# Query tiles and softmax reciprocals fetched by one 128-partition transfer each, with the queries' scratch rows laid out for it

## The chip, the core and the metric

The kernel runs on one core of a Trainium2 chip. The core has five engines that each run their own instruction list in order: TensorE (PE in the profile, with its weight loads shown apart as PEld), VectorE (DVE), ScalarE (ACT), GpSimd (POOL) and SyncE (SP). In this kernel SP computes nothing: it issues nearly every DMA, one after the other, and where a DMA has to wait for something, SP waits and all later DMAs stand behind it. The data of a DMA is then moved by 16 DMA engines that the whole core shares. The metric is the time on the device, in microseconds (us), as the median of 3 runs.

## What is computed

It is one step of a two-layer backbone on 1024 latent and 256 context tokens, 1280 in all, or ten tiles of 128 rows. Layer 0 is an attention layer, layer 1 a Fourier layer. Of the attention layer the following matters here:

```python
qa, ka, va, ga, qb, kb, vb, gb = split_even(h @ w_in)      # 8 q heads, 2 kv heads, head_dim 64, twice
qa = rms_norm(qa.reshape(b, s, A_HEADS, HEAD_DIM), gq)     # mixer A, then rotary positions
...
oa = dense_block_attention(qa, ...)                        # mixer A: all keys
ob = window_attention_with_ctx(qb, ..., sink)              # mixer B: +-128 tokens, context, sink
return jnp.concatenate([oa * jax.nn.silu(ga), ob * jax.nn.silu(gb)], axis=-1) @ w_out
```

A softmax divides by the sum of its exponentials. The kernel does not divide in the attention: it keeps the sums, turns them into reciprocals, and multiplies a whole row tile by reciprocals and gates just before the output projection.

## The kernel before

All matrix products run in a split format: an operand is kept as a high part and a low part, so one product is two or three matmuls. PE is the busy engine nearly everywhere.

The stretch that the change touches is layer 0, from the first query projections to the output projections.

**Queries out.** `q_pair` (from L773) makes the queries of two row tiles for one group of four heads. There are four groups `g` (0 and 1 of mixer A, 2 and 3 of mixer B) and five pairs of tiles, so twenty calls. After normalisation and rotary positions, its inner `post` transposes the result on PE, splits it into `qe` (high and low), and writes each of the two tiles to a scratch tensor in DRAM, `qd` (L185). The write at L803 takes 128 partitions of 512 numbers (2 KB). The partitions are two heads of 64 dimensions each, `(h d)`, and `qd` holds them in that order, `[NT, 4, 128, 512]`. There are 40 such writes.

**Queries in.** `load_q` (L926 to L930) fetches a tile's queries for one group. The keys occupy the 128 partitions as high part over low part (64 dimensions each), so the queries are wanted twice, once for each half of the partitions, and both heads side by side in a partition. Two transfers do that (L929): each fills 64 partitions with two rows of 2 KB. There are 40 tile loads, so 80 transfers. The buffers come from a zone named `q` with two places, which also lends places to `qe` and to other tiles. `attend` (from L1077) loads the next tile's queries during the first half of the present tile, so there is one tile of lookahead.

**Scores and weighing.** `soft` computes the scores of two heads at a time (L924, L996), `weigh` transposes the probabilities, multiplies by the values and writes the result to the scratch tensor `od` (L1064). Between these units a `Filler` hands out other PE work: the remaining projections and the gates. `totals` (L1012 on) writes the reciprocals of a tile to the scratch tensor `scd` (L1028).

**Into the output projection.** `proj_in` (from L1206) loads for one row tile the attention output (L1210), the gates (L1213) and the reciprocals (L1215). A reciprocal belongs to a head, and a head's 64 dimensions are 64 partitions, so the row of each of the two heads in a partition block is broadcast to 64 partitions, in two transfers of 64 rows of 4 KB. There are 10 row tiles, so 20 transfers.

The order of the instructions is not that of the code: a scheduler orders each engine's list ahead of time by its own model of durations. So the written form of a DMA can also move other instructions. The rows of `qd` and `scd` reach PE through these waits: a store into `qd` must have landed before its load is issued, a load must have landed before the tile's first score matmul, and a reciprocal load must have landed before the multiplication at L1216, on which the output projection rests.

Of the kernel before, what the change touches and what calls it, by code (L numbers as in the profile page):

```python
# [9 lines left out]
F32 = mybir.dt.float32  # L10
# [7 lines left out]
P = 128  # L18
D = 1024
NT = 10  # L20
# [119 lines left out]
def hybrid_step(ctx: ExitStack, tc: tile.TileContext, I, O):  # L140
    nc = tc.nc
    pe, act, dve, pool, sp = nc.tensor, nc.scalar, nc.vector, nc.gpsimd, nc.sync
# [3 lines left out]
    dr = ctx.enter_context(tc.tile_pool(name="dram", bufs=1, space=bass.MemoryType.DRAM))  # L146
# [9 lines left out]
    def take(tag, shape, dt=F32):  # L156
        tags = (tag,) if isinstance(tag, str) else tag
        z = min((t for t in tags if spare[t]), key=lambda t: spare[t][0])
        i = spare[z].popleft()[1]
        size = 2 if dt == BF16 else 4  # L160
        for s in shape[1:]:
            size *= s
        assert size <= 4 * ZONES[z][1]
        made[0] += 1
        return Buf(z, i, up.tile(list(shape), dt, tag=f"{z}{i}", name=f"{z}{made[0]}", bufs=1))

    def drop(*bufs):
        for b in bufs:
            stamp[0] += 1
            spare[b.zone].append((stamp[0], b.idx))  # L170

    def bank(tag, name, dt=F32):
        tag = ALIAS.get(tag, tag)
        return pp.tile([P, 512], dt, tag=tag, name=name, bufs=BANKS[tag])
# [7 lines left out]
        ring.rotate(-1)  # L182
        return bank(ring[-1], name)

    qd = dr.tile([NT, 4, P, 512], F32, name="qd")  # L185
    kd = dr.tile([2, P, NT * P], F32, name="kd")
    vd = dr.tile([2, NT, P, P], F32, name="vd")
    od = dr.tile([NT, P, 8, P], F32, name="od")
# [4 lines left out]
    scd = dr.tile([NT, 2, 8, P], F32, name="scd")  # L193
# [74 lines left out]
    def pick(key, cycle):  # L268
        turn[key] = turn.get(key, -1) + 1
        return {"d": dve, "p": pool, "a": act}[cycle[turn[key] % len(cycle)]]  # L270

    def copy(key, cycle, out, in_):
        e = pick(key, cycle)
        if e is act:
            act.activation(out, in_, AF.Copy)  # L275
        else:
            e.tensor_copy(out, in_)  # L277
# [395 lines left out]
    def transp(name, y, n):  # L673
        tp = t_bank(name)
        for i in range(n):
            pe.transpose(tp[:, i * P : i * P + P], y[:, i, :], ident)
        return tp
# [18 lines left out]
    def rope_pair(y, n, t, t1, t2):  # L696
        cb = rope[:, t : t + 2, 0:32].unsqueeze(2).to_broadcast([P, 2, 2 * n, 32])
        pick("rope", XE["rope"]).tensor_mul(  # L698
            t1.rearrange("p t h (b c) -> p t (h b) c", b=2), y.rearrange("p t h (b c) -> p t (h b) c", b=2), cb
        )  # L700
        for b in range(2):
            o, i = 32 * b, 32 - 32 * b
            sb = rope[:, t : t + 2, 32 + o : 64 + o].unsqueeze(2).to_broadcast([P, 2, n, 32])
            pick("rope", XE["rope"]).tensor_mul(t2[:, :, :, o : o + 32], y[:, :, :, i : i + 32], sb)
        pick("radd", XE["radd"]).tensor_add(t1, t1, t2)

    def norm_pair(name, src, y, sq, n, g, post=None):
        act.activation(sq, src, AF.Square)
        ss2 = sm.tile([P, 8], F32, tag="hssq", name=name + "ssq")[:, 0 : 2 * n]
        dve.tensor_reduce(out=ss2.rearrange("p (t h) -> p t h", t=2), in_=sq, op=ALU.add, axis=AX.X)  # L710
        rs = rsqrt(name + "rs", ss2, 2 * n, 1.0 / 64, post, pw=XE["pw"])
        rb = rs.rearrange("p (t h) -> p t h", t=2).unsqueeze(3).to_broadcast([P, 2, n, 64])
        dve.tensor_mul(y, y, rb)
        pick("gm", XE["gm"]).tensor_mul(y, y, g.unsqueeze(1).unsqueeze(1).to_broadcast([P, 2, n, 64]))

    def gemm_tok(acc, t, w, n=256):
        mm3(acc, [(*htile(t, k), *wk(w, k, 0, n)) for k in range(8)])
# [55 lines left out]
    def q_pair(m, kv, t, w, ptag, acc=None):  # L773
        if acc is None:
            acc = bank(ptag, f"q{m}{kv}{t}")
            for i in range(2):
                gemm_tok(acc[:, i * 256 : i * 256 + 256], t + i, w)
        yb = take(HZ[0], (P, 2, 4, 64))
        y = yb.a
        av = acc.rearrange("p (t h d) -> p t h d", t=2, h=4)  # L780
        act.activation(y, av, AF.Copy, scale=1.0 if m == 0 else 0.125)  # L781
        b1 = take(HZ[0], (P, 2, 4, 64))
        b2 = take(HZ[0], (P, 2, 4, 64))
        if m == 0:
            norm_pair(f"qn{kv}{t}", av, y, b2.a, 4, gq, 0.125)
        if t < 8:
            rope_pair(y, 4, t, b1.a, b2.a)
            y = b1.a
        if t < 8:
            drop(yb, b2)  # L790
            qb = b1
        else:
            drop(b1, b2)
            qb = yb

        def post():
            tp = transp(f"qT{m}{kv}{t}", y.rearrange("p t (a h) d -> p (t a) (h d)", h=2), 4)
            tv = tp.rearrange("p (t n) -> p t n", t=2)
            qe = take(QE_Z, (P, 2, 2, 256), F32R)
            copy("qev", E_QEV, qe[:, :, 0, :], tv)  # L800
            dve.tensor_sub(qe[:, :, 1, :], tv, qe[:, :, 0, :])
            for i in range(2):
                sp.dma_start(qd[t + i, 2 * m + kv], qe[:, i].rearrange("p a n -> p (a n)").bitcast(F32))  # L803
            drop(qe, qb)

        return post
# [118 lines left out]

    def load_q(t, g):  # L926
        q = take("q", (P, 2, 512))
        for i in range(2):
            sp.dma_start(q[64 * i : 64 * i + 64], qd[t, g].rearrange("(h d) f -> d h f", d=64))  # L929
        return q  # L930

    def soft(t, g, pr, qb):
# [140 lines left out]
    def flush_held(n=0):  # L1073
        while len(held) > n:
            held.popleft()()
# [59 lines left out]
    for i, nm in enumerate(order[:-1]):  # L1135
        j = int(nm[-1])
        work = []
        if nm[0] == "q":
            m = "ab".index(nm[1])
# [66 lines left out]
    def proj_in(src, gate, r, resid):  # L1206
        if gate is not None:
            flush_held()
            ol = take(OB[0], (P, 8, P))
            sp.dma_start(ol.a, src[r])  # L1210
            gl = take(OB[0], (P, 8, P))
            rl = take(OB[0], (P, 8, P))
            sp.dma_start(gl.a, gate[r])  # L1213
            for h in range(2):
                sp.dma_start(rl[64 * h : 64 * h + 64], scd[r, h].partition_broadcast(64))  # L1215
            pick("pm", XE["pm"]).tensor_mul(gl.a, gl.a, rl.a)  # L1216
            pick("pm", XE["pm"]).tensor_mul(ol.a, ol.a, gl.a)
            drop(gl, rl)
        hi, lo = take(OB[0], (P, 8, P), F32R), take(OB[0], (P, 8, P), F32R)
        if gate is not None:  # L1220
            split(hi.a, lo.a, ol.a, E_OH, E_OL)
            drop(ol)
        else:
            for c in range(2):
                split(hi[:, 4 * c : 4 * c + 4, :], lo[:, 4 * c : 4 * c + 4, :], src(c, r), "a", "d")
        xr = take(OB[0], (P, D))
        sp.dma_start(xr.a, resid[r * P : (r + 1) * P, :])
        return hi, lo, xr
# [426 lines left out]
    for n in range(4):  # L1655
        c, hf = divmod(n, 2)
# [306 lines left out]
```

## Time and profile before

| what | value |
|---|---|
| median of 3 runs (lowest to highest) | 1202.58 us (1201.54 to 1202.74) |
| the profiled execution's own time | 1202.03 us |
| its span, first to last instruction | 1200.2 us |
| PE busy | 1162.1 us, 97% of the span |
| DVE busy | 831.7 us, 69% |
| ACT busy | 578.5 us, 48% |
| POOL busy | 319.1 us, 27% |
| DMA: bytes moved, packets | 168.81 MB, 129840 |
| share of the 16 DMA engines' span taken by the SP queue's packets | 45.8% |

The profiled execution lies 0.55 us under the median, inside the spread of the runs. Between its time and its span there are 1.8 us that lie around the instructions. A share of DMA is a mean over the 16 engines: 0.45 of a stretch of 100 us means that each engine was busy for 45 us of it on average. The table gives averages over stages that differ much; the stretch from 100 to 830 us is the one with the attention layer.

### The profile page before, as it was taken

To read this page: it belongs to the slowest core of one execution; us is meant where nothing else is said; L and a number is where in the kernel's file an instruction comes from. 1 tells how busy PE (TensorE), PEld (TensorE's weight loads), DVE (VectorE), ACT (ScalarE), POOL (GpSimd) and SP (SyncE) were. 2 spreads that over 40 slices of the span, in tenths; PEclk is the share of its full clock that TensorE was granted. 3 is DMA by queue.
4 is the path that set the end of the run, shared out by engine and by line. 5 is a ranking of instruction groups with operands and counts; after the bars stand their busy time and mean duration, and the time that the engine had idled before them with its cause. 6 is when DMAs were issued, how large, how long until landed. Compare 5 with 4: busy or idle time off the path is not lost. (4 is left out here: it accounts for less than half of the span.)

```text
span 1200.2 us, 22028 instructions
## 1 busy us (share of the span) xinstructions
PE 1162.1 (97%) x8103; PEld 1038.7 (87%) x8103; DVE 831.7 (69%) x2000; ACT 578.5 (48%) x1159; POOL 319.1 (27%) x278
## 2 busy tenths in 40 slices
PE   7899899999999999999999979999999999999997
PEld 5787899999999999899988978888878888997886
DVE  3479688877677776678888957678756953467543
ACT  3343356665566555556666756433363224342211
POOL 2255554411322221010110113312212217345001
PEclk9899999999999999999999989999999999999999
DMA  9957512323623232354353587587114436264321
GB/s 316 370 188 255 162 52 64 113 76 88 169 69 104 75 95 76 90 127 123 79 151 80 159 232 223 184 253 248 54 45 158 137 110 181 86 206 147 123 105 54
DMA packets 129840, 168.81 MB, mean 141 GB/s; under 512 B 26298, under 2 KB 86454, under 8 KB 129732
## 3 DMA queue, kind: packets, MB, share of 16 engines
q1 hardware_dynamic: 129732, 167.40, 45.8%
q8 instruction: 64, 1.05, 0.4%
q14 instruction: 44, 0.36, 0.1%
HBM read 123.19 MB, written 44.16 MB: 139 GB/s over the span
## 5 line engine op out<-in xcount | busy, mean ns | idle before, releaser
L1044 DVE TENSOR_TENSOR pt<-pt,pt 128x512 fp32r<-128x512 f32 (+1 forms) x264 | 171.6, 659 | 45.0 <-ACT pt L275 44.2
L275 ACT ACTIVATE pt<-pt 128x512 fp32r<-128x512 f32 (+1 forms) x264 | 146.9, 575 | 95.8 <-PE pt L1041 56.7
L1047 PE MATMUL av<-pt,u 128*128 128x256 f32 x1008 | 165.6, 287 | 0.1
L1041 PE MATMUL pt<-identr,p 128*128 128x128 f32 x1008 | 154.6, 272 | 0.4 <-DVE pt L1044 0.3
L263 PE MATMUL q<-w,u 128*128 128x256 f32 x960 | 144.5, 288 | 0.2 <-ACT h L725 0.2
L1047 PEld LDWEIGHTS av<-pt,u 128*128 128x128 f32 x1008 | 138.1, 189 | 3.7 <-DVE pt L1044 0.8
L263 PEld LDWEIGHTS q<-w,u 128*128 128x128 f32 x960 | 127.5, 190 | 5.9 <-issue 0.8
L1041 PEld LDWEIGHTS pt<-identr,p 128*128 128x128 f32 x1008 | 118.9, 140 | 7.0 <-PE sB L996 0.9
L263 PE MATMUL ga<-u,w 128*128 128x512 f32 (+1 forms) x576 | 124.5, 360 | 0.3 <-DVE h L817 0.3
L965 ACT ACTIVATE p<-p,nm 128x1280 f32<-128x1280 f32 (+1 forms) x80 | 95.4, 1193 | 58.1 <-DVE p L958 57.8
L263 PEld LDWEIGHTS ga<-u,w 128*128 128x128 f32 x576 | 93.9, 188 | 14.5 <-ACT e L1056 0.5
L281 POOL TENSOR_TENSOR w<-h,w 128x512 fp32r<-128x512 f32 x39 | 52.3, 1357 | 129.6 <-DVE w L277 100.3
L924 PE MATMUL sL<-u,q 128*128 128x512 f32 x256 | 82.9, 411 | 0.3 <-DMA q<-qd 0.3
L281 POOL TENSOR_TENSOR u<-h,u 128x512 fp32r<-128x512 f32 x24 | 34.8, 1458 | 163.5 <-ACT u L275 151.9
L965 ACT ACTIVATE p<-p,NM 128x640 f32<-128x640 f32 (+2 forms) x80 | 59.1, 740 | 24.9 <-DVE p L958 24.5
L924 PE MATMUL sC<-u,q 128*128 128x256 f32 x320 | 63.4, 299 | 6.9 <-DMA q<-qd 6.6
L958 DVE TENSOR_SCALAR_CACHE_REDUCE p<-sL 128x512 f32<-128x512 f32 x64 | 43.9, 685 | 27.0 <-PE sL L924 17.5
L263 PE MATMUL oz<-u,u 128*128 128x512 f32 x208 | 59.6, 396 | 0.1
L263 PE MATMUL oz<-u,w 128*128 128x512 f32 x192 | 58.2, 395 | 0.0
L924 PEld LDWEIGHTS sC<-u,q 128*128 128x128 f32 x320 | 48.6, 191 | 9.7 <-issue 7.0
L958 DVE TENSOR_SCALAR_CACHE_REDUCE p<-sL,nm 128x512 f32<-128x512 f32 x64 | 47.7, 745 | 11.8 <-PE sL L924 10.9
L698 POOL TENSOR_TENSOR h<-h,rope 128x512 f32<-128x512 f32 (+1 forms) x18 | 21.6, 1199 | 125.7 <-ACT h L781 67.9
(738 smaller groups left out, 2568.5 us busy)
## 6 DMA issues: line engine op xcount, KB each, us to landing
q<-qd SPq DMA_DIRECT2D x80, 256.0 KB
p<-i_ada_w SPq DMA_DIRECT2D x20, 512.0 KB
h<-i_w_in SPq DMA_DIRECT2D x40, 256.0 KB
h<-i_w_out SPq DMA_DIRECT2D x32, 256.0 KB
pt<-i_ada_w SPq DMA_DIRECT2D x15, 512.0 KB
qd<-pt SPq DMA_DIRECT2D x20, 256.0 KB
q<-i_ada_w SPq DMA_DIRECT2D x9, 512.0 KB
qd<-q SPq DMA_DIRECT2D x18, 256.0 KB
```

The source lines that it names most:

```text
L263: pe.matmul(out, a, b, start=i == 0, stop=i == n - 1)
L275: act.activation(out, in_, AF.Copy)
L281: pick("lo" + lc, lc).tensor_sub(dst_l, src, dst_h)
L698: pick("rope", XE["rope"]).tensor_mul(t1.rearrange("p t h (b c) -> p t (h b) c", b=2), y.rearrange("p t h (b c) -> p t (h b) c", b=2), cb)
L924: pe.matmul(ps, q_at(q, s, hc), keys, start=s == 0, stop=s == 1)
L958: dve.tensor_scalar(p[i][:, end[i] : end[i] + n], ps, sign, last[i], op0=ALU.mult, op1=ALU.min, accum_out=c)
L965: act.activation(p[i][:, 0 : end[i]], p[i][:, 0 : end[i]], AF.Exp, bias=last[i], scale=-1.0, accum_out=SU[:, t, hd + i, 0:1],)
L1041: pe.transpose(tp[:, jj * 256 + i * P : jj * 256 + i * P + P], p[i][:, off : off + P], ident)
L1044: dve.tensor_sub(pt[:, 1, 0:n], tp[:, 0:n], pt[:, 0, 0:n])
L1047: pe.matmul(acc, vv, pt[:, s, jj * 256 : jj * 256 + 256], start=c + jj + s == 0, stop=c + jj == nt - 1 and s == 1,)
```

## The change

The scratch tensor `qd` becomes `[NT, 4, 64, 1024]`: a row is now one of the 64 dimensions, with both heads side by side. The store writes the same 128 partitions, but to a target that is walked as two heads of 64 rows. The load becomes one transfer: the whole block of 64 rows of 4 KB is named twice, by a leading step of zero with a count of 2, and fills all 128 partitions. The load of the reciprocals likewise becomes one transfer, whose source is two rows, each repeated 64 times.

```diff
-    qd = dr.tile([NT, 4, P, 512], F32, name="qd")
+    qd = dr.tile([NT, 4, 64, 1024], F32, name="qd")
...
             for i in range(2):
-                sp.dma_start(qd[t + i, 2 * m + kv], qe[:, i].rearrange("p a n -> p (a n)").bitcast(F32))
+                dst = qd[t + i, 2 * m + kv].rearrange("d (h f) -> h d f", h=2)
+                sp.dma_start(dst, qe[:, i].rearrange("p a n -> p (a n)").bitcast(F32))
...
     def load_q(t, g):
         q = take("q", (P, 2, 512))
-        for i in range(2):
-            sp.dma_start(q[64 * i : 64 * i + 64], qd[t, g].rearrange("(h d) f -> d h f", d=64))
+        sp.dma_start(q.a.rearrange("p h f -> p (h f)"), qd[t, g].partition_broadcast(2))
         return q
...
-            for h in range(2):
-                sp.dma_start(rl[64 * h : 64 * h + 64], scd[r, h].partition_broadcast(64))
+            sp.dma_start(rl.a.rearrange("p c n -> p (c n)"), scd[r].rearrange("h c n -> h (c n)").unsqueeze(1).broadcast_to((2, 64, 1024)))
```

So three access patterns get a slowest (outermost) count of 2 on their DRAM side: the store's target (2 x 64 x 512), the query load's source (2 x 64 x 1024, with a step of 0 for the 2) and the reciprocal load's source (2 x 64 x 1024, with a step of 0 for the 64). On the SBUF side the outermost count is 128 in all three. Before, the outermost counts of these transfers were 128 for the store and 64 for both kinds of load, on both sides.

The scheduler's lists change from about the hundredth microsecond on. Three places show it.

The first is SP's list early in the attention, where the first query tiles are loaded and more are stored. Before (a name is a buffer: `q_` is a query tile, `qd` and `od` are the scratch tensors, `h_` a raw piece of weights, `e_` an attention output):

```order
L929 DMA q_1675<-qd 64x2x512 x2
L929 DMA q_1870<-qd 64x2x512 x2
L296 DMA h_2200<-i_w_in 128x2x256
L296 DMA h_2204<-i_w_in 128x2x256
L1064 DMA od<-e_1769 64x2x128
L803 DMA qd<-pt_2013 128x512 x2
L1064 DMA od<-e_1936 64x2x128
L803 DMA qd<-q_2183 128x512 x2
L1064 DMA od<-e_2110 64x2x128
L929 DMA q_2237<-qd 64x2x512 x2
```

The same stretch of SP's list in the changed kernel:

```order
L929 DMA q_1674<-qd 128x1x1024
L929 DMA q_1868<-qd 128x1x1024
L296 DMA h_2197<-i_w_in 128x2x256
L296 DMA h_2201<-i_w_in 128x2x256
L1064 DMA od<-e_1767 64x2x128
L804 DMA qd<-pt_2010 2x64x512 x2
L1064 DMA od<-e_1933 64x2x128
L804 DMA qd<-q_2180 2x64x512 x2
L929 DMA q_2234<-qd 128x1x1024
L1064 DMA od<-e_2107 64x2x128
```

Each pair of query loads has become one; the row shows the target, whose outermost count is 128. The stores' target now stands with an outermost count of 2. One load has moved ahead of one small store of attention output.

The second place is PE's list where the scores of the very first tile begin (`sL` are the scores, `ad` the products for the other layer's conditioning, `q_` here the accumulator of a query projection). Before:

```order
L467 MATMUL ad_1467<-p_1486,e_114 32x128 x8
L467 MATMUL ad_1467<-p_1496,e_114 32x128 x8
L467 MATMUL ad_1467<-pt_1506,e_114 32x128 x8
L924 MATMUL sL_0000_1650<-u_888,q_1643 128x512 x2
L263 MATMUL q_1939<-w_542,u_498 128x256
```

And in the changed kernel:

```order
L925 MATMUL sL_0000_1649<-u_888,q_1643 128x512 x2
L467 MATMUL ad_1467<-p_1486,e_114 32x128 x8
L467 MATMUL ad_1467<-p_1496,e_114 32x128 x8
L467 MATMUL ad_1467<-pt_1506,e_114 32x128 x8
L925 MATMUL sL_0001_1653<-u_888,q_1643 128x512 x2
```

The first scores, which need the first query load, now stand ahead of 24 conditioning matmuls that do not need it, and the second scores stand right behind those.

The third place is SP's list late in the attention layer, where three row tiles of the output projection are prepared (`scd` are the reciprocals, `gd` the gates). Before:

```order
L1028 DMA scd<-e_10124 16x128
L1215 DMA u_10497<-scd 64x1024 x2
L1215 DMA w_10315<-scd 64x1024 x2
L1064 DMA od<-e_10111 64x2x128
L1213 DMA w_10314<-gd 128x1024
L1210 DMA q_10418<-od 128x1024
L1215 DMA p_10421<-scd 64x1024 x2
```

And in the changed kernel:

```order
L1028 DMA scd<-e_10080 16x128
L1337 DMA x1d<-w_9513 128x1024
L1064 DMA od<-e_10067 64x2x128
L1210 DMA q_10373<-od 128x1024
L1214 DMA p_10376<-scd 128x1x1024
L1214 DMA u_10451<-scd 128x1x1024
L1214 DMA w_10271<-scd 128x1x1024
```

The three reciprocal loads of these tiles now stand directly behind each other, with the load of attention output ahead of them.

## The prediction

> **What bounds the kernel now.** I read the page first:
>
> ```profile
> span 1200.2 us, 22028 instructions
> PE 1162.1 (97%) x8103; PEld 1038.7 (87%) x8103; DVE 831.7 (69%) x2000; ACT 578.5 (48%) x1159; POOL 319.1 (27%) x278
> DMA packets 129840, 168.81 MB, mean 141 GB/s; under 512 B 26298, under 2 KB 86454, under 8 KB 129732
> ```
>
> PE has work for all but 38 us, so shorter transfers can give back little. Then the busy time by stages (columns: stage, its length, busy time and instructions of PE, PEld, DVE, ACT and POOL, the granted clock, the mean busy share of the 16 DMA engines, GB/s):
>
> ```profile
> 100.00:300.00 200.00, 194.58 (x1698) 183.45 (x1697) 159.49 (x385) 106.31 (x185) 80.79 (x79) 0.99 0.37 110
> 300.00:510.00 210.00, 209.74 (x1585) 198.42 (x1583) 152.35 (x372) 120.43 (x216) 45.31 (x38) 1.00 0.35 97
> 510.00:690.00 180.00, 178.57 (x1197) 162.63 (x1196) 148.12 (x465) 117.25 (x272) 19.77 (x16) 1.00 0.46 120
> 690.00:830.00 140.00, 132.86 (x728) 114.32 (x728) 99.92 (x241) 67.61 (x149) 34.54 (x17) 0.98 0.75 223
> ```
>
> In these 730 us PE is busy for 715.8, so 14.2 us is all that any reordering or faster DMA could gain there. The DMA engines are busy for a third to a half of it, and for three quarters at the end. Last, PE's waits between 100 and 830 us (total, times, longest):
>
> ```profile
> PE sC L924 <- DMA q<-qd: 6.6, 1, 6.6
> PE ad L467 <- DMA p<-i_ada_w: 3.1, 1, 3.1
> ...
> PE sL L924 <- DMA q<-qd: 0.3, 1, 0.3
> ```
>
> Of 40 tile loads one makes PE wait in earnest. The two stretches of 10 us around it:
>
> ```profile
> 700.00:710.00 10.00, 9.62 (x67) 8.92 (x65) 8.34 (x25) 6.76 (x16) 0.86 (x1) 1.00 0.98 292
> 710.00:720.00 10.00, 3.79 (x11) 3.28 (x12) 3.84 (x10) 4.31 (x10) 3.82 (x2) 0.67 0.73 214
> ```
>
> A load that queues behind full DMA engines (0.98) stops PE at once, because only one tile of queries is fetched ahead. So the queries are hidden as long as they land quickly, and the question is what the new form does to the landing.
>
> **What the change removes.** The transfers by stage (issue time min/median/max in ns, first and last issue). Loads of queries are halves of tiles before:
>
> ```profile
> L803 SPq DMA_DIRECT2D qd<-q x10: 319/381/1428, 120.5 to 267.7; - x10
> L803 SPq DMA_DIRECT2D qd<-pt x8: 325/384/426, 166.5 to 235.7; - x8
> L803 SPq DMA_DIRECT2D qd<-p x2: 422/475/528, 108.6 to 109.2; - x2
> L929 SPq DMA_DIRECT2D q<-qd x18: 573/599/1464, 116.9 to 279.5; - x18
> ...
> L803 SPq DMA_DIRECT2D qd<-pt x12: 325/384/432, 336.4 to 454.8; - x12
> L803 SPq DMA_DIRECT2D qd<-q x8: 319/382/1614, 372.6 to 469.1; - x8
> L929 SPq DMA_DIRECT2D q<-qd x22: 586/603/1228, 303.1 to 507.0; - x22
> ...
> L929 SPq DMA_DIRECT2D q<-qd x29: 573/598/987, 518.2 to 683.0; - x29
> ...
> L929 SPq DMA_DIRECT2D q<-qd x11: 586/598/608, 690.7 to 750.8; - x11
> L1215 SPq DMA_DIRECT2D u<-scd x16: 444/538/602, 695.7 to 825.7; - x16
> L1215 SPq DMA_DIRECT2D w<-scd x2: 536/562/588, 780.0 to 780.5; - x2
> L1215 SPq DMA_DIRECT2D p<-scd x2: 451/522/594, 783.2 to 783.7; - x2
> ```
>
> 40 query issues and 10 reciprocal issues go, about 0.6 us of SP's time each, 30 us. SP computes nothing, so this shortens nothing by itself; at most a load starts 0.6 us sooner. That is worth something only at the 6.6 us wait.
>
> **What it does to the transfers themselves.** Three clean bursts give the price of the bytes: a tile's two half loads (first row), two stores (second), and for comparison 128 rows of 4 KB in one transfer, an output store (third); their windows are 3, 2 and 2 us long, and no other packet lies in them:
>
> ```profile
> DMA packets 288, 0.52 MB, mean 175 GB/s; under 512 B 32, under 2 KB 32, under 8 KB 288
> ...
> q1 hardware_dynamic: 288, 0.52, 64.4%
> ```
>
> ```profile
> DMA packets 288, 0.52 MB, mean 262 GB/s; under 512 B 32, under 2 KB 32, under 8 KB 288
> ...
> q1 hardware_dynamic: 288, 0.52, 70.5%
> ```
>
> ```profile
> DMA packets 144, 0.52 MB, mean 262 GB/s; under 512 B 16, under 2 KB 16, under 8 KB 144
> ...
> q1 hardware_dynamic: 144, 0.52, 65.1%
> ```
>
> Engine time is share x 16 x window: 30.9 us for a tile's two loads, 22.6 us for two stores (11.3 each), 20.8 us for 512 KB in 4 KB rows. Beside 256 or 128 rows of data each burst has 16 packets under 512 B per transfer: I read these as one closing packet from each DMA engine that took part. Where a pattern has only 4 rows (two stores from L1644 and L1645, alone in a window but for the beginning of a weight load), there are 4 for each, 8 in all:
>
> ```profile
> DMA packets 43, 0.08 MB, mean 51 GB/s; under 512 B 8, under 2 KB 12, under 8 KB 43
> ```
>
> So the number of engines follows the counts of the access pattern, not a fixed 16. Every large transfer of the kernel before has an outermost count of 128, 64 or 16. The change gives all 90 of its transfers an outermost count of 2 on the DRAM side. My forecast is that each of them then runs on two engines, and always the same two, with the other 14 idle for it. What the row with 4 leaves open is whether 64 inner rows would be spread after all, since its four rows had only four packets to hand out.
>
> [...]
>
> The price on two engines: a load of 512 KB in 4 KB rows takes 20.8 / 2 = 10.4 us, against 30.9 / 16 = 1.93 us for the pair now. If it kept the 30.9 of the pair, it would be 15.5 us; I take 10.4, because the pair's packets were slowed by all 16 engines reading at once. A reciprocal load has the same bytes and rows: 10.4 us. A store takes 11.3 / 2 = 5.64 us, against 0.705.
>
> Since every other transfer also has a sixteenth of its bytes on these two engines, they become a queue that all share. Its work by stage, with the rest taken as share x length less the old part of these transfers:
> - 100 to 300: 20 stores 112.8 + 9 tile loads 93.6 + rest 42.5 (74.0 - 14.1 - 17.4) = 248.9 us in 200, 48.9 too many.
> - 300 to 510: 20 stores 112.8 + 11 loads 114.4 + rest 38.2 (73.5 - 14.1 - 21.2) = 265.4 in 210, 55.4 too many.
> - 510 to 690: 14.5 loads 150.8 + rest 54.8 (82.8 - 28.0) = 205.6 in 180, 25.6 too many.
> - 690 to 830: 5.5 tile loads and 10 reciprocal loads 161.2 + rest 75.1 (105.0 - 29.9) = 236.3 in 140, 96.3 too many.
>
> That is 956.2 us of work in 730, an excess of 226.2 us if the two engines never pause. They do pause: a tile's load can only be issued when its buffer is free, that is when the tile before is scored. How long nothing of it runs is seen here, where the two issues begin at 144.98 and their packets all lie after 146.2:
>
> ```profile
> 144.98 1.22 SPq L929 DMA_DIRECT2D q<-qd  x2
> ```
>
> 1.2 us for each of 40 tiles is 48 us. Behind the waiting instruction stands, on PE, all filler that could have run meanwhile, since PE's list is fixed and its score matmuls now even stand ahead of 24 conditioning matmuls; on SP, the stores, weights and attention outputs stand behind whichever load waits for its buffer. The moved instructions themselves I set at nothing: the lists of PE hold the same matmuls, and the 14.2 us of PE's idle time bound what their order could give.
>
> Sum, from the profiled execution's own 1202.0 us: 1202.0 + 226.2 + 48 = **1476 us**. That execution lies 0.6 us under the median of the runs, which is nothing here. A change of 0.2% (2.4 us) is about what a measurement of this kernel can tell from none.
>
> **The rivals.**
>
> *The new form is spread over all 16 engines* (the hardware divides the 64 inner rows): the other side. For it: the row with 4 closing packets had no inner rows to divide, and the target's outermost count is still 128. Then a tile costs 20.8 engine-us in place of 30.9, one issue goes, and the 6.6 us wait can vanish: 1202.0 - 6.6 = 1195 at best, 1202 if the load is late for the same queue, since at 0.98 the wait is made by the transfers ahead of it. I take 1198. It decides as long as a load lands within the tile before it, 180 / 14.5 = 12.4 us from 510 to 690. [...]
>
> *Two engines, but the attention hides them until 690 us.* From 510 to 690 a load takes 10.4 us of a tile's 12.4, so each load alone fits, and the stores before 510 may be absorbed by waiting buffers. Then only the last stage pays: 1202.0 + 96.3 = 1298 us. Against it: the sums of all four stages are over their lengths, and the queue is served in order.
>
> *Every load fully exposed.* If the load always starts only when PE has run dry, the 50 loads cost 50 x 10.4 = 520 us: 1722. Against it: the load is issued a tile ahead now, and early in the attention a tile takes 200 / 9 = 22 us, twice a load's time.
>
> **How the numbers follow.** Two engines with a shared queue, about 1476: 0.73. Spread over 16: 0.10 (faster 0.06, within 0.2% 0.03, slower 0.01). Hidden until 690: 0.10. Fully exposed: 0.07. The three slow cases and that 0.01 make slower 0.91.
>
> The range: at the low end I take in the second rival, 1298. At the high end the two engines are packed no better than all 16 were around the one wait, (0.98 + 0.73) / 2 = 0.855: 956.2 / 0.855 = 1118, an excess of 388, and with the 48 this is 1638; 15.5 us a load would go beyond it but only with a price I hold unlikely, and PE's clock, which fell to 0.67 where it idled, pushes the same way. I say 1298 to 1640. Outside lie the first and third rivals, 0.17, and a little of the forecast's own ends.
>
> **What would show it.** If two engines carry these transfers, the number of packets is 40 x 130 + 40 x 130 + 10 x 130 in place of 80 x 144 + 40 x 144 + 20 x 80: 129840 falls by 7180 to about 122660, and those under 512 B fall from 26298 to about 24240. Spread over 16 they would be 123920 and about 25500. PE's waits for `q<-qd` become the longest row, some 150 us or more; PE's share falls to 1162 / 1474 or 79%; the stage of the output projections waits for `scd`; a lone query load lies in a window of more than 10 us at a share of about 0.125. The mean DMA share over the whole span hardly grows though the DMA is the bound: that mean hides two full engines behind 14 empty ones. I am wrong if a query load lands within 3 us, or if the loads take 10 us and PE still does not wait. I am wrong in size, not in kind, if the waits fall only after 690 us or if stores, not loads, are what the waits name.

## The result, and the profile after

The changed kernel takes 1625.43 us (1623.58 to 1626.90, four runs); the kernel before, on the same chip, 1202.46 us (1201.54 to 1202.74). The ratio is 1.352, 95% interval 1.350 to 1.354: slower by 423 us, where 274 were forecast. The head of the page of the changed kernel, with the SP queue's row:

```profile
span 1624.6 us, 21961 instructions
...
PE 1251.7 (77%) x8103; PEld 1110.0 (68%) x8103; DVE 838.4 (52%) x2000; ACT 578.1 (36%) x1159; POOL 317.2 (20%) x278
...
DMA packets 122660, 168.80 MB, mean 104 GB/s; under 512 B 24238, under 2 KB 84394, under 8 KB 122552
...
q1 hardware_dynamic: 122552, 167.39, 31.8%
```

The same 8103 matmuls and the same megabytes, in 424.4 us more. PE idles for 1624.6 - 1251.7 = 372.9 us, against 38.1 before: +334.8. The other 89.6 us are PE's own busy time, which grew from 1162.1. The packets are the forecast 122660, and those under 512 B miss the forecast 24240 by two. The queue's share of 16 engines fell from 45.8% to 31.8%, although the DMA now holds everything up.

That a transfer runs on two engines can be seen directly in a quiet stretch of 10 us. Its windows row (columns as in the prediction: length, PE, PEld, DVE, ACT, POOL, granted clock, share of 16 engines, GB/s), and what moved in it:

```profile
576.00:586.00 10.00, 4.66 (x37) 4.24 (x35) 3.18 (x9) 1.46 (x2) 0.00 (x0) 0.83 0.12 49
```

```profile
DMA packets 120, 0.49 MB, mean 49 GB/s; under 512 B 0, under 2 KB 0, under 8 KB 120
...
q1 hardware_dynamic: 120, 0.49, 12.1%
```

A query load was issued at 574.24 and two stores just behind it. In the 10 us no transfer ends (no packet under 512 B), and 12.1% of 16 engines is 1.94 engines: two are full, 14 do nothing. 1.94 x 10 / 120 is 0.161 us a packet, so the 130 packets of a load take 0.161 x 130 / 2 = 10.5 us, as the prediction had it (10.4). The two stores, issued at 575.25 and 575.80, have their first packet at 586.58, as the load's 128 rows end (they run from 575.56 to 586.59, the first two in over 1.0 us each): the stores are on the same two engines and are served after the load. Meanwhile PE works for 4.66 us of the 10.

Who waits, over the whole run (total, times, longest):

```profile
ACT pt L275 <- DMA qd<-pt: 138.5, 10, 21.8
...
PE sC L925 <- DMA q<-qd: 84.7, 11, 16.4
...
PE sL L925 <- DMA q<-qd: 78.7, 9, 10.6
PE av L1047 <- ACT pt L275: 77.9, 11, 17.7
...
ACT u L275 <- DMA h<-i_w_out: 62.8, 15, 11.5
...
DVE e L1058 <- DMA od<-e: 38.8, 7, 18.8
...
POOL u L1215 <- DMA u<-scd: 32.0, 1, 32.0
```

PE waits for queries for 163.4 us in 20 waits, in place of 6.9 in two. But the longest row that names a DMA is not a load: ACT waits 138.5 us to refill a `pt` buffer whose queries are still being stored, and PE's products `av` wait 77.9 us for ACT. The wait for `h<-i_w_out`, output weights that the change does not touch, was 20.1 us before. The SP queue itself stands longer, too. A query load can't be issued before its store has landed, and while SP waits for that, every later DMA stands behind it:

```profile
SPq L929 <- DMA qd<-q: 93.0, 10, 12.9
```

Before, this row was 8.4 us.

Where in the kernel: the score matmuls of mixer A (`sL`) and of both mixers (`sC`), with the shortest, median and longest in ns, first and last start, before and then after:

```profile
L924 PE MATMUL sC<-u,q x320: 276/282/552, 132.2 to 782.5; 128*128 128x256 f32 x160
...
L924 PE MATMUL sL<-u,q x256: 387/396/796, 127.0 to 505.9; 128*128 128x512 f32 x128
```

```profile
L925 PE MATMUL sC<-u,q x320: 274/282/584, 147.3 to 1155.0; 128*128 128x256 f32 x160
...
L925 PE MATMUL sL<-u,q x256: 387/397/797, 138.4 to 728.0; 128*128 128x512 f32 x128
```

Up to the first score it is 11.4 us more; mixer A takes 728.0 - 138.4 = 589.6 us in place of 378.9 (+210.7); from there to the last score 427.0 in place of 276.6 (+150.4); behind it 469.6 in place of 417.7 (+51.9). Where PE idles more, the granted clock is lower. Two stretches of the attention and the one behind it, after:

```profile
300.00:500.00 200.00, 145.29 (x1021) 138.14 (x1020) 98.41 (x244) 76.67 (x142) 27.29 (x31) 0.85 0.22 68
...
900.00:1100.00 200.00, 124.20 (x726) 112.52 (x724) 92.58 (x275) 77.09 (x180) 18.14 (x10) 0.80 0.30 95
...
1250.00:1625.00 375.00, 353.81 (x2042) 300.71 (x2040) 214.67 (x405) 124.69 (x262) 100.92 (x86) 0.98 0.37 121
```

In these two stretches of the attention PE works for 73% and 62% of the time, at a granted clock of 0.85 and 0.80; in the attention before, the clock was 0.98 to 1.00. Behind the attention it is 0.98 again. The median `sL` matmul is as fast as before (397 ns, 396 before), but more of them are slow, as the mean of each group shows, before and after (busy us, mean ns of one):

```profile
L924 PE MATMUL sL<-u,q 128*128 128x512 f32 x256 | 82.9, 411 | 0.3 <-DMA q<-qd 0.3
```

```profile
L925 PE MATMUL sL<-u,q 128*128 128x512 f32 x256 | 92.3, 454 | 82.5 <-DMA q<-qd 78.7 <-DVE p L958 2.0 <-DVE pt L1044 1.8
```

Of the 256 `sL` matmuls 41 now take over 600 ns, up to 797 ns or twice the median, where 2 did before; 40 of the 41 lie in stretches in which the trace's clock record has half the clock (0.50). There are 43 such stretches, 402 us in all, and PE is busy for 192.6 us of them. If work takes twice as long there, 96.3 us of PE's busy time are lost to the clock; the same sum is 10.1 us before. The difference, 86.2 us, is nearly all of the 89.6 us by which PE's busy time grew.

### The profile page after: what moved, and what is told of

Its sections match the earlier page's. It is cut to its first block, busy times and chain, and to the rows that moved or that the text cites. A ratio compares the mean times of both kernels' runs of the same rounds, so it can differ in the third digit from the quotient of the medians.

```text
span 1624.6 us, 21961 instructions
## 1 busy us (share of the span) xinstructions
PE 1251.7 (77%) x8103; PEld 1110.0 (68%) x8103; DVE 838.4 (52%) x2000; ACT 578.1 (36%) x1159; POOL 317.2 (20%) x278
## 2 busy tenths in 40 slices
DMA packets 122660, 168.80 MB, mean 104 GB/s; under 512 B 24238, under 2 KB 84394, under 8 KB 122552
## 3 DMA queue, kind: packets, MB, share of 16 engines
q1 hardware_dynamic: 122552, 167.39, 31.8%
## 5 line engine op out<-in xcount | busy, mean ns | idle before, releaser
L1047 PE MATMUL av<-pt,u 128*128 128x256 f32 x1008 | 187.1, 312 | 98.2 <-ACT pt L275 77.9
L275 ACT ACTIVATE pt<-pt 128x512 fp32r<-128x512 f32 (+1 forms) x264 | 147.6, 575 | 267.2 <-DMA qd<-pt 138.5
L1047 PEld LDWEIGHTS av<-pt,u 128*128 128x128 f32 x1008 | 155.4, 210 | 106.2 <-ACT pt L275 80.2
L1041 PE MATMUL pt<-identr,p 128*128 128x128 f32 x1008 | 170.4, 290 | 0.6 <-DVE pt L1044 0.5
L263 PE MATMUL q<-w,u 128*128 128x256 f32 x960 | 157.1, 305 | 7.5 <-ACT h L708 7.2
L925 PE MATMUL sL<-u,q 128*128 128x512 f32 x256 | 92.3, 454 | 82.5 <-DMA q<-qd 78.7
L263 PEld LDWEIGHTS q<-w,u 128*128 128x128 f32 x960 | 140.1, 207 | 13.7 <-ACT h L708 7.4
L263 PE MATMUL ga<-u,w 128*128 128x512 f32 (+1 forms) x576 | 130.1, 373 | 10.4 <-DVE h L818 10.2
L1041 PEld LDWEIGHTS pt<-identr,p 128*128 128x128 f32 x1008 | 129.4, 150 | 7.8 <-DVE pt L1044 1.3
L925 PEld LDWEIGHTS sL<-u,q 128*128 128x128 f32 x256 | 45.2, 211 | 87.9 <-issue 74.9
L263 PE MATMUL oz<-u,u 128*128 128x512 f32 x208 | 64.7, 425 | 35.5 <-DVE h L1237 35.5
L1058 DVE TENSOR_TENSOR e<-av,e 64x256 f32<-64x256 f32 x80 | 32.9, 411 | 82.8 <-ACT e L1056 41.8
L263 PEld LDWEIGHTS oz<-u,u 128*128 128x128 f32 x208 | 42.1, 206 | 46.3 <-DVE h L1237 29.4
```

The source lines that it names most:

```text
L263: pe.matmul(out, a, b, start=i == 0, stop=i == n - 1)
L925: pe.matmul(ps, q_at(q, s, hc), keys, start=s == 0, stop=s == 1)
L1041: pe.transpose(tp[:, jj * 256 + i * P : jj * 256 + i * P + P], p[i][:, off : off + P], ident)
L1047: pe.matmul(acc, vv, pt[:, s, jj * 256 : jj * 256 + 256], start=c + jj + s == 0, stop=c + jj == nt - 1 and s == 1,)
L1058: dve.tensor_add(os_[..., ::-1] if rev else os_.a, a3[0:64], lo_sb.a)
```

## The experiments

The theory to test: every transfer with an outermost count of 2 runs on two DMA engines, and everything else is done late because of that. Rivals: the new layout of the scratch rows costs by itself; one transfer to 128 partitions is worse than two to 64 whatever its count; one of the three edits makes nearly all of the loss. And within the theory it was open how the time is lost: by two engines with more work than a stage is long (the prediction's sum), by the late landing of the load itself, or by everything else that stands behind. Each time is compared with runs of the kernel before on the same chip (1198.5 to 1200.2 us there). All kernels compute the whole reference.

**The layout alone.** The new rows of `qd`, but stores and loads in two halves of 64 partitions each, so that all counts are 64; the reciprocals as before.

```diff
+                for h in range(2):
+                    src = qe[64 * h : 64 * h + 64, i].rearrange("p a n -> p (a n)").bitcast(F32)
+                    sp.dma_start(qd[t + i, 2 * m + kv][:, 512 * h : 512 * h + 512], src)
...
+        for i in range(2):
+            sp.dma_start(q[64 * i : 64 * i + 64].rearrange("p h f -> p (h f)"), qd[t, g])
```

> The new scratch layout (64 rows of 4 KB) is kept, but every store and every load of queries is written as two transfers of 64 partitions, so that no pattern has an outermost count of 2; the reciprocals stay as before. Theory A (an outermost count of 2 puts a transfer on two DMA engines, and nothing else matters): 1195 to 1206 us, and 16 closing packets for every transfer, so the packets under 512 B are 26298 + 40 x 16 = 26938. Theory B (the new layout and the order that the scheduler makes of it cost the time): the better part of the 423 us remains, over 1400 us.

1203.74 us, ratio 1.0054 (1.0032 to 1.0075); PE waits for `sC<-q` 8.6 us. The layout is not the cause. Rows of 4 KB in place of 2 KB for the loads gain nothing either.

**The parts by themselves.** Only the stores in one transfer with a target of 2 x 64 rows (the two blocks 72 rows apart); only the loads, from the new layout with stores in halves; only the reciprocals.

```diff
+    qd = dr.tile([NT, 4, 2, 72, 512], F32, name="qd")
...
+                dst = qd[t + i, 2 * m + kv][:, 0:64]
+                sp.dma_start(dst, qe[:, i].rearrange("p a n -> p (a n)").bitcast(F32))
```

> The kernel before, with only the stores of queries on a target whose outermost count is 2: the same rows of 2 KB in the same order, the two heads' blocks 8 unused rows apart so that they cannot be named as 128 rows. Loads and reciprocals as before. Theory A: two engines, 5.64 us a store; the packets under 512 B fall by 40 x 14 = 560 to 25738. By the queue's sum the two engines have 345 us of work in the 410 us up to 510, so no excess; what it costs comes from the buffers that a store holds longer (the three of the zone of the transposed probabilities above all): 1220 to 1330 us. Theory B: 1200 to 1206, since layout and row sizes stay.

> Only the query loads on two engines: new layout, stores in two transfers of 64 partitions, loads in one transfer as in the changed kernel, reciprocals as before. Theory A: a load lands 12.4 us after its issue; by the queue's sum some 37 us are too many after 510 us, and 28 of the 40 loads had less than 12.4 us between issue and first use, 106 us short in all: 1290 to 1350 us, PE's wait for query loads over 90 us. Theory B (layout and order): about as slow as the changed kernel, over 1450, or as fast as the halves, depending on the order alone.

> The kernel before with only the reciprocals in one transfer as in the changed kernel; queries as before. Theory A: ten loads of 10.4 us on two engines between 690 and 830 us; the two engines have there 104 + 86 = 190 us of work in 140: about +50 us, 1225 to 1260 us; packets under 512 B 26298 - 320 + 20 = 25998. Theory B: 1198 to 1206 us.

Stores: 1328.33 us, 1.108 (1.106 to 1.111), +130. Loads: 1386.72, 1.157 (1.154 to 1.160), +188. Reciprocals: 1276.78, 1.065 (1.063 to 1.067), +78. The loads and the reciprocals lost more than was expected of them. Together it is +396 of the 423, so the three add up nearly and none carries the loss alone. The packets and the waits of each, stores first:

```profile
DMA packets 129280, 168.80 MB, mean 127 GB/s; under 512 B 25738, under 2 KB 85894, under 8 KB 129172
```

```profile
ACT pt L275 <- DMA qd<-pt: 101.4, 10, 13.7
...
PE av L1048 <- ACT pt L275: 59.9, 9, 10.7
...
PE sL L925 <- DMA q<-qd: 11.4, 3, 4.7
```

Then the loads:

```profile
PE sC L926 <- DMA q<-qd: 78.9, 11, 13.6
...
ACT u L275 <- DMA h<-i_w_out: 62.8, 14, 11.8
...
PE sL L926 <- DMA q<-qd: 26.1, 7, 7.0
```

And the reciprocals:

```profile
PE oz L263 <- DVE h L1237: 35.8, 3, 26.4
...
DVE e L1058 <- DMA od<-e: 27.3, 3, 15.6
...
DVE u L1215 <- DMA u<-scd: 19.2, 1, 19.2
```

Each part brings one of the rows that the changed kernel shows. With 40 stores on two engines in place of 16 the small packets fall by 26298 - 25738 = 560 = 40 x 14.

**One transfer with a higher count.** First the reciprocals: every row is stored eight times, so that the one load of 128 partitions has an outermost count of 16.

```diff
+            src = scd[r].rearrange("h j c n -> (h j) (c n)").unsqueeze(1).broadcast_to((16, 8, 1024))
+            sp.dma_start(rl.a.rearrange("p c n -> p (c n)"), src)
```

> Reciprocals in one transfer to 128 partitions as in the changed kernel, but with an outermost count of 16: each reciprocal row lies eight times in the scratch tensor (written so by two small stores in place of one), and the load repeats each of the 16 rows for 8 partitions. Queries as before. Theory A: 1195 to 1208 us, where the same transfer with a count of 2 cost 78 us. Theory B (one transfer is slow as such, or the scheduler's order is): 1250 or more.

1201.91 us, 1.0025 (1.0007 to 1.0043): the form is the change's own, and with 16 in place of 2 its +78 us are gone. Then the query loads: each row is stored twice, as four blocks of 32 rows that lie 40 rows apart, so that the one load has a count of 4. In the control the blocks touch, which makes the load 128 plain rows; the stores are the same four of 32 partitions in both. First the kernel with a count of 4 against the kernel before, then the control against the kernel with a count of 4:

```diff
+    qd = dr.tile([NT, 4, 4, 40, 1024], F32, name="qd")
...
+        sp.dma_start(q.a.rearrange("p h f -> p (h f)"), qd[t, g, :, 0:32])
```

```diff
-    qd = dr.tile([NT, 4, 4, 40, 1024], F32, name="qd")
+    qd = dr.tile([NT, 4, 4, 32, 1024], F32, name="qd")
...
-        sp.dma_start(q.a.rearrange("p h f -> p (h f)"), qd[t, g, :, 0:32])
+        sp.dma_start(q.a.rearrange("p h f -> p (h f)"), qd[t, g].rearrange("a d f -> (a d) f"))
```

> Query loads in one transfer of 128 rows of 4 KB, whose source has an outermost count of 4: the scratch block of a tile is four blocks of 32 rows, 8 unused rows apart, and holds every row twice; four stores a tile from 32 partitions each write a row to both places. Reciprocals as before. Theory A (the count sets the engines): four engines, 5.2 us a load, landing some 7 us after the issue; 9 of the 40 loads of the kernel before had less than that between issue and first use, 18 us short in all: 1205 to 1245 us, against the 188 us of the loads on two engines. Packets under 512 B: 26298 - 40 x 16 + 160 x 16 - 80 x 16 + 40 x 4 = 27098. Theory B (one transfer for both halves is slow as such): about as slow as the loads on two engines, 1350 or more.

> Control for the run with loads of four blocks. Queries are stored twice, by the same four stores of 32 partitions a tile, but the blocks are not padded, so that the load is 128 plain rows of 4 KB with an outermost count of 128. If the count of 4 made that run's +98 us, this one is within 1.5% of before (1185 to 1217 us). If the 160 small stores and the extra bytes made it, this one is at 1270 or more. In between, each has its part. In both cases I expect the count of packets under 512 B to be 40 x 12 = 480 above that run's 27098, 27578, and none of the waits of PE for the queries above 15 us in total under the first theory.

A count of 4: 1297.29 us, 1.083 (1.079 to 1.087), outside what was expected. A count of 128: 1200.83, 1.001 (0.999 to 1.003). So the extra stores and bytes cost nothing, and the whole +98 us belongs to the loads on four engines. The packets, 4 first and 128 second:

```profile
DMA packets 130641, 179.30 MB, mean 139 GB/s; under 512 B 27098, under 2 KB 87254, under 8 KB 130532
```

```profile
DMA packets 131121, 179.30 MB, mean 150 GB/s; under 512 B 27578, under 2 KB 87734, under 8 KB 131012
```

Twelve closing packets fewer for each of the 40 loads: 4 where there were 16. PE's waits for the queries in the run with 4:

```profile
PE sC L928 <- DMA q<-qd: 26.5, 7, 6.6
...
PE sL L928 <- DMA q<-qd: 9.0, 4, 2.5
```

That is 35.5 us of the 98. By its count such a load takes half of 10.4 us, 5.2 as an estimate, and by the prediction's table no stage would overflow: from 510 to 690, the tightest, 14.5 x 5.2 + 54.8 = 130 us of work on each of the four engines in 180 us. Yet half of the +188 remains. A load's last semaphore update came 9.0 us after its issue in the median, where the control has 3.9 and some 7 was expected. The sum over stages was not how the time is lost.

**What the change sets out to do, on 16 engines.** Both steps together: queries stored twice by two stores of 64 partitions and loaded by one transfer of 128 plain rows, reciprocals with a count of 16.

> What the change sets out to do, on all 16 DMA engines: queries are stored twice (each row of 4 KB once for either half of the partitions, by two stores of 64 partitions), so that a tile's load is one transfer of 128 plain rows; the reciprocals' rows are stored eight times, so that their one load has an outermost count of 16. If the loss of the changed kernel is the count of 2 alone, this kernel is within 0.7% of before (1190 to 1208 us), packets under 512 B near 27480, and its wait for the queries under 15 us. If one transfer to 128 partitions in place of two to 64 is by itself what costs (all rows to one engine in turn, no overlap of two transfers), it is at 1280 or more. A gain of over 0.3% would say that the 50 issues and the second reading of the same rows were worth something; since PE was idle for 38 us and 7 of them for queries, I expect none.

1208.01 us, 1.007 (1.005 to 1.009), at the edge of what was expected. There is no gain. What 50 issues fewer would be worth by themselves, the run does not show, since the extra stores bring as many back: it issues 714 DMAs, the kernel before 708. By the profile of before it is nothing (SP computes nothing, PE idled 7 us for queries). Why this kernel is 0.7% slower and not level was not followed up. No version tried beats the kernel before.

**Where the stores hurt.** With the stores on two engines ACT waited for `pt`, and SP stood for 80.1 us at query loads whose rows had not landed. To see if it is that zone of three buffers, `qe` is split into two tiles of the zone `h`, with the stores on two engines and, as control, as before.

```diff
-            qe = take(QE_Z, (P, 2, 2, 256), F32R)
...
+            qes = [take("h", (P, 2, 256), F32R) for i in range(2)]
...
```

> The stores on two engines as in e2_stores2, but the split queries stand in two tiles of 2 KB from the zone of nine small buffers, and no longer in one of the three buffers of the transposed probabilities. Theory A1 (the stores cost because they hold those three buffers, for which ACT and then PE wait): ACT's waits for them go, and of the 130 us of e2_stores2 less than 60 are left over the control. Theory A2 (the two engines' queue itself costs the 130 us): 90 us or more are left.

> Control for e7: the kernel before with the split queries in the zone of small buffers, all transfers on 16 engines as before. Both theories: 1195 to 1215 us; the copies are 40 of half the size in place of 20.

Stores on two engines: 1284.32 us, 1.072 (1.068 to 1.076). Control: 1207.20, 1.007 (1.005 to 1.010). So 77 us of the 130 stay, which lies between the two expectations. The waits of the first:

```profile
DVE w L277 <- DMA h<-i_w_in: 63.0, 13, 12.5
...
PE av L1049 <- DVE pt L1046: 26.7, 4, 11.2
```

The row of ACT waiting for `qd<-pt` is gone, and DVE waits for weights instead, 63.0 us against 13.1 in the control. Freeing one kind of buffer takes back 53 us. Part of what stays is a held buffer again: the raw weights come from the zone `h` too, and SP waits at their loads until a store has given its buffer back:

```profile
SPq L296 <- DMA qd<-h: 71.8, 12, 11.2
```

In the control this row is 9.7 us. So the run does not tell how much of the stores' loss is held buffers and how much the two engines' queue.

**Late, or occupied?** Two runs were made to part these. In the first the transfers are those of before, but each loaded query tile is multiplied by 1.0 four times on POOL before its use: late queries and a quiet DMA.

```diff
+        for i in range(4):
+            pool.tensor_scalar(q.a.bitcast(F32R), q.a.bitcast(F32R), 1.0, None, op0=ALU.mult)
```

> Lateness without a busy DMA queue: the kernel before with its transfers as they are, but each loaded query tile is multiplied by 1.0 in place four times on POOL before its first use, some 2.4 us each (a 128x1024 operation of POOL in the trace of before), so about 9.6 us a tile and 385 us of POOL in all. This is about the lateness of a load on two engines (10.4 us in place of 1.9). If lateness at PE and the slower clock that follows from its pauses make the +188 us of the kernel with loads on two engines, this kernel is at +120 us or more, and PE's busy time grows by 20 us or more though no DMA engine carries more. If what costs is that other transfers stand behind the loads on the two shared engines, it is at +60 us or less. POOL's other work stands behind the four operations, which works for the first theory and so weakens a high result, not a low one.

In the second the queries come promptly on 16 engines, and behind each load stands a copy on two engines that nobody on PE needs. It goes over the rows of the tile loaded before, so it can't run ahead of the loads.

```diff
+        seen.append((t, g))
+        if len(seen) > 1:
+            sp.dma_start(qd[seen[-2]][:, :, 0:1024], qd[t, g, 0, :, 0:1024].partition_broadcast(2))
```

> Occupation without lateness: queries are stored and loaded in halves on 16 DMA engines as in the kernel with halves (new layout, 1.0054 of before), and behind each tile's load but the first stands one more transfer, a copy in DRAM of that tile's queries with an outermost count of 2 (128 rows of 4 KB), for which nothing on PE waits: 39 copies that keep two DMA engines busy about as the loads on two engines did, and where they did. Nothing of the computation is left out. If most of the +188 us of the kernel with loads on two engines comes from the landing of the load itself, 10.4 us after its issue in place of 2, this kernel is at +60 us or less (1205 to 1260). If it comes from all other transfers standing behind the loads with their sixteenth of the bytes, it is at +120 us or more, and PE or the engines ahead of it wait for weights, stores and attention outputs. Packets should be 125360 + 39 x 130 = 130430, those under 512 B 26938 + 39 x 2 = 27016, if the copies run on two engines.

Late queries: 1346.17 us, 1.122 (1.120 to 1.124), +146. Copies: 1431.34, 1.194 (1.190 to 1.198), +233. Neither is small. In the run with late queries POOL is busy for 760.9 us in place of 319.1, and hardly any of PE's idle time carries the name of the queries:

```profile
span 1345.8 us, 22230 instructions
...
PE 1219.8 (91%) x8103; PEld 1058.7 (79%) x8103; DVE 848.4 (63%) x2000; ACT 577.3 (43%) x1159; POOL 760.9 (57%) x438
```

```profile
POOL q L931 <- DMA q<-qd: 91.4, 21, 15.6
...
PE sC L924 <- POOL q L931: 12.4, 7, 3.9
```

The four operations took 2.79 us each (446.1 us for 160), 11.2 us a tile, and POOL stood at them for 91.4 us waiting for loads, with its other work behind. PE's busy time grew by 57.7 us without any change to the DMA, at a mean clock of 0.966. The run shows that such lateness can cost this much; it does not say how much of the loads' +188 it is, since POOL's queue has its share. In the run with copies:

```profile
DMA packets 130432, 189.26 MB, mean 132 GB/s; under 512 B 27017, under 2 KB 87173, under 8 KB 130323
```

```profile
DVE e L1064 <- DMA od<-e: 70.0, 13, 8.4
...
ACT u L276 <- DMA h<-i_w_out: 64.7, 16, 15.7
...
ACT pt L276 <- DMA qd<-pt: 48.7, 9, 9.6
...
PE av L1053 <- DVE e L1064: 41.5, 11, 8.3
...
PE sC L927 <- DMA q<-qd: 38.5, 9, 11.1
```

Transfers with all 16 engines to run on, for attention outputs, weights, stores and queries, wait here, and the 39 copies cost more than the 40 loads on two engines. But a copy does more than occupy two engines. SP stands at it until the query load in front of it has landed, with all later DMAs behind:

```profile
SPq L935 <- DMA q<-qd: 126.3, 37, 11.8
```

No run has the same copies on 16 engines, so the +233 us are the price of both together. A copy also keeps the engines a little longer; one that was alone in its window:

```profile
DMA packets 54, 0.22 MB, mean 39 GB/s; under 512 B 0, under 2 KB 0, under 8 KB 54
...
q1 hardware_dynamic: 54, 0.22, 11.2%
```

The window is 5.6 us long: 0.112 x 16 x 5.6 / 54 = 0.186 us a packet, or 12.1 us a copy, against 10.5 a load. Scaled by that, 233 becomes 202 us, still above 188.

That two full engines hold up the other transfers can be seen without this comparison. The trace keeps the semaphore updates by which a transfer tells of its landing: 16 for each of the 128 stores of attention output, whose count is 64, and for a query load with a count of 2 one about 1 us after its issue and two more at its end. When the 14th and the 16th update of a store of attention output came after its issue (us, medians):

| run | 14th | 16th |
|---|---|---|
| before | 2.48 | 2.78 |
| late queries, all transfers as before | 2.25 | 2.34 |
| copies on two engines | 2.58 | 5.29 |
| loads alone on two engines | 2.27 | 5.37 |
| the changed kernel | 2.44 | 9.04 |

Fourteen parts land as before, and two land late wherever transfers run on two engines. In the run with the loads alone, the load's own last update comes 13.4 us after its issue (3.9 before). So both readings are true of the same run: the load is late, and so is what shares its engines. How the +188 us divide between them, and SP's waits, stays open.

## Why the prediction was right in kind and short in size

- *Two engines for a count of 2: right.* The packet counts came out to within two, the quiet window shows 1.94 engines, and the parts and the counts of 4, 16 and 128 agree: with 128 partitions on the SBUF side, DRAM-side counts of 2, 4, 16 and 128 came with 2, 4, 16 and 16 closing packets a load. That a count of 2 on one side alone gives two engines, and always the same two, was the author's estimate; no row of before has a large transfer with such a count. The changed kernel showed the two engines, and in the quiet window the same two for a load and the stores behind it. One transfer to 128 partitions in place of two to halves found no gain here at 16 engines: ratios 1.0025, 1.001 and 1.007, though each of these kernels also stores its rows several times.
- *10.4 us a load: right* (10.5 in the quiet window). The reason given for it over 15.5, that 16 engines reading at once slow the packets, was the author's estimate; no run was made to test it.
- *The rivals:* spreading over 16 and hiding until 690 us fell. Mixer A, which ended at 506 us before, already lost 211 us. The fully exposed case, 1722, was too much.
- *The excess over stages, 226.2 us: a sum that fitted badly.* It says that time is lost only where two engines have more to do than the stage is long. For the stores alone its own numbers give 112.8 + (74.0 - 14.1) = 172.7 us of work in 200 and 112.8 + (73.5 - 14.1) = 172.2 in 210, so no excess at all; the run lost 130 us. For the loads on four engines no stage is full either; the run lost 98.
- *The pauses, 40 x 1.2 = 48 us: the step that failed.* The attention now runs from 100 to about 1250 us (the last load of reciprocals is issued at 1246.2), and the 956.2 us of work that the prediction laid on the two engines fill 0.83 of these 1150. That leaves 194 us of pause. The trace's packets bear it out: for 182.6 us of the 1150 no packet runs on any engine, and for 23.7 us only one, so for 206 us the two engines are not both at work. Against 48 that is about the whole miss (1624.6 against a forecast span of 1474). The prediction's 1.2 us stood only for the time from issue to first packet. What it left out is the other direction: while the two engines are full, stores hold `pt` buffers (ACT waits 138.5 us), attention outputs hold `e` (DVE waits 38.8), weights come late (62.8, before 20.1), SP stands at loads whose rows have not landed (93.0, before 8.4), and PE stops (163.4 at queries). That a stopped PE then also frees no buffer for the next load is argued, not shown by a row.
- *The high end, 1638, came near by luck.* Its packing of 0.855 was read from 20 us around one wait on 16 engines, and the 48 us of pauses stand on top of it, although a packing below 1 is a pause already.
- *"The stores may be absorbed by waiting buffers"*, said of the second rival: they were not. Three `pt` buffers and stores on two engines give the longest row after that names a DMA (138.5 us), and 101.4 us of waiting in the run with stores alone.
- *PE's clock, named at the high end and not priced: 86 us* of PE's time, as worked out with the profile after; most of the rest of the 424 us is PE's added idling, 334.8 us. The granted clock went from 0.989 to 0.877, and the mean `sL` matmul from 411 to 454 ns. In the runs of single parts PE's busy time grew too: 27.8 us beside 99.3 of added idling (stores), 42.0 beside 143.2 (loads), 13.3 beside 59.8 (reciprocals). That is 0.22 to 0.29 us for each that PE idles, but no rule: it is 0.37 with the copies (61.7 beside 167.9) and 0.48 with loads on four engines (30.4 beside 63.1). All 43 stretches of reduced clock in the changed kernel are at 0.50; from 586 to 600 us, for one, PE works for 3.69 of 14 us at a granted clock of 0.50. Of the 35 pauses of PE and its weight loads over 4 us all touch such a stretch, of the eight of 2 to 4 us two do. But nine of the 43 stretches touch no pause of 1 us, so which pause brings the lower clock is not shown.
- *The signs:* PE's share was 77% (79 forecast), its waits for queries 163 us (150 or more), the `scd` wait came, and the DMA's mean share did not grow but fell. The sign set for "wrong in size", that the waits name stores, came in part: the longest single row that names a DMA is that of the `pt` buffers, though PE's waits for loads are longer in sum.
- *The moved instructions, set at nothing:* not tried apart. The kernels with 16 engines have orders of their own too and lie within 0.8% of before, so there is no sign that order mattered.

## What to carry to other kernels

Before two transfers are merged into one, look at the outermost count of both sides of the new pattern. Here a leading count of 2, also one with a step of zero or one that a rearranged target brought in, put each transfer on two of 16 engines (1.94 busy in the quiet window). The price was not the 10.5 us of the load itself, and not the overflow of a queue alone: the last of the 16 parts of a store of attention output landed 9.04 us after the issue in place of 2.78, short buffer zones and in-order lists stopped although the two engines were not both at work for 206 us of 1150, and PE's granted clock was 0.877 in place of 0.989. When a queue is sized, ask of each buffer zone how long it is held, and of each DMA that waits what stands behind it in the issuing list. Reckon with a PE that may slow too: here its busy time grew by 0.2 to 0.5 us for each that it idled more behind late DMAs.

## What the runs showed that was not expected

- Four engines were nowhere near enough: loads of 512 KB at a count of 4 cost +98 us, half of the +188 at a count of 2, with the DMA's mean rate at 139 GB/s, against 150 in the control with the same stores.
- The mean DMA share said little of what was late. It fell from 45.8% to 31.8%, while for 589 us of the 1150 of the attention exactly two packets were under way; the count of packets under 512 B told it at once.
- 39 copies whose data nothing uses cost 233 us (1.194), with SP's waits at them included.
- PE's busy time grew by 57.7 us in the run with late queries, where no DMA engine carried more. Half-clock stretches explain 22.3 us of it by the sum above (64.7 us of busy time in them, 20.1 before); what made the rest stays open.
